# Parking two residual blocks in DRAM from the weights' queue, in program order, in a macaron decoder layer

## The chip, the cores and the metric

The kernel runs on one core of a Trainium2 chip. The metric is the device time of one execution in microseconds (us): three runs of the kernel before took 1733.95, 1736.27 and 1739.5, so the median is 1736.27. The profile is of one further execution, recorded by the hardware profiler; its times are counted from the start of its span.

Engines are named as the profile names them: PE is TensorE's matmul, PEld its load of the stationary operand, DVE is VectorE, ACT is ScalarE, POOL is GpSimd, SP is SyncE. SP issues DMAs only, and its queue carries the weights. POOL issues DMAs too, in a queue of its own. L845 is line 845 of the kernel before.

## What is computed

A decoder layer on x of 256 rows by 2048 columns in float32: half a SwiGLU, a mixer (gated linear attention in 4 heads beside dilated attention in 8), and half a second SwiGLU, each on the RMS norm of x and each added to x. The change is in the second SwiGLU.

```python
def rms_norm(x, g):
    y = x * lax.rsqrt(jnp.mean(x * x, axis=-1, keepdims=True) + EPS)
    return y * g

def swiglu(x, w_gate, w_up, w_down):          # 2048 -> 5632, twice, and 5632 -> 2048
    return (jax.nn.silu(x @ w_gate) * (x @ w_up)) @ w_down

x = x + 0.5 * swiglu(rms_norm(x, ffn1_norm), ffn1_w_gate, ffn1_w_up, ffn1_w_down)
z = rms_norm(x, mix_norm) @ w_in
...
x = x + jnp.concatenate([o_g, o_a], axis=-1) @ w_out
x = x + 0.5 * swiglu(rms_norm(x, ffn2_norm), ffn2_w_gate, ffn2_w_up, ffn2_w_down)
```

## The kernel before

**Tiles.** The 256 rows are two blocks of 128 (t = 0, 1), which stay in SBUF as the tile xs (128 partitions, block, 2048 columns). The normed activations are held transposed in hh and hl: hh is the value rounded to the fast matmul type fp32r, hl what the rounding left. A product of float32 is three matmuls, L274 (high by high), L276 (high activations by low weights) and L278 (low by high), all into one PSUM bank.

**Weights.** They come from DRAM in tiles of 1 MB (raw, three buffers), by SyncE's queue, L217, one after the other for the whole kernel. ScalarE rounds each half of a tile to wh (L113), VectorE subtracts to get wl (L114); wh and wl have four buffers each. Halves are prepared up to two ahead of the matmuls that take them. A raw buffer is free for the next tile when both of its halves are split.

**Norm.** Ahead of the second SwiGLU each 512-column piece of xs is transposed into hh and hl. Pieces 0 and 1 of each block go by norm_moved: VectorE transposes 32x32 squares (L128), GpSimd moves the squares by 16 small DMAs for each piece (move_squares, L133, here hh<-us), and VectorE multiplies with the gain when they have landed (L153). Pieces 2 and 3 go by norm_block: TensorE transposes into a PSUM bank (L109), VectorE multiplies out of it (L123), and both kinds are then split (L113, L114). Row factors come from GpSimd's power (L165).

**Gate and up of the second SwiGLU.** ffn runs 11 column blocks of 512 columns. Block 0 is plain (column_pair): for each of 16 row pieces it takes a half tile of weights and issues the matmuls of both token blocks. A dictionary called extra gives work to issue ahead of a step of this loop. Blocks 1 to 10 form part of their products with seven multiplications in place of eight (L298 to L300); for these, the sums of activations (seven_forms, L316 to L322, with split to fh and fl) and of weights (L238 and those behind it) need scratch. That scratch is xs itself: xs[:, 1, :] holds the sums, and half of xs[:, 0, :] takes the squares that GpSimd moves for the transposed outputs (xs<-us, L133). So the second SwiGLU first has to save xs, the residual, in a DRAM tile named resid, and GpSimd reads it back ahead of the down projection (L465 for block 1, L470 for block 0).

**Order.** Each engine runs its instructions in one order, which the scheduler of the tile framework sets from the program and from the dependencies it sees; an instruction may so stand elsewhere than in the code. keep_in_program_order pins an instruction to its place in the program among its queue's. Whoever overwrites a part of xs has to wait until the DMA that reads it has landed: L316 for block 1, L133's moves of block 1's outputs for block 0. The first SwiGLU has a like place: load_x (L523) loads xs by SyncE's queue, L524, in program order, at steps 9 and 11.

Of the kernel before, what the change touches and what calls it, by code (L numbers as in the profile page):

```python
# [21 lines left out]
P = 128  # L22
# [5 lines left out]
NT = S // P  # L28
# [20 lines left out]
def layer_kernel(tc, x, xT, gains, gla_gate_up, gla_gate_bias, gla_out_norm, att_q_norm, att_k_norm,  # L49
                 w_ff1, w_dn1, w_mix, w_low, w_out, w_ff2, w_dn2, c_sq, c_rope, c_mask, out):  # L50

    nc = tc.nc
# [3 lines left out]
    with ExitStack() as es:  # L56
# [35 lines left out]
        xs = cst.tile([P, NT, D], F32, name="xs")  # L92
# [749 lines left out]
            eng.dma_start(out[t * P:(t + 1) * P, c * 512:(c + 1) * 512], blk)  # L842

        resid = es.enter_context(tc.tile_pool(name="dram", bufs=1, space=bass.MemoryType.DRAM)).tile([S, D], F32, name="resid")
        ffn("ffn2", done2, resid, extra={9 + t: lambda t=t: nc.gpsimd.dma_start(resid[t * P:(t + 1) * P, :], xs[:, t, :]) for t in range(NT)}, final=True)  # L845


# [73 lines left out]
```

## Time and profile before

| | |
|---|---|
| three runs, us | 1733.95, 1736.27, 1739.5 |
| profiled execution, us | 1733.12 |
| its span, us | 1731.3 |
| ACT busy, us | 940.0 (54%) |
| POOL busy, us | 442.4 (26%) |
| weight tiles of 1 MB by SP's queue | 175 + 88 + 48 + 16 |
| SP's queue, share of the 16 DMA engines' time | 55.6% |
| POOL's queue, the same | 4.3% |
| DMA rate over the span, GB/s | 207 |

The profile lists busy time by engine, the chain of work that ended last, groups of instructions with the idle time ahead of them and what ended it, and the DMA issues with their time to landing. A releaser behind "<-" is what a wait ended with. The changed place lies at about 1070 us; the down projection of the second SwiGLU ends the kernel.

### The profile page before, as it was taken

To read this page: it belongs to the slowest core of one execution; us is meant where nothing else is said; L and a number is where in the kernel's file an instruction comes from. 1 tells how busy PE (TensorE), PEld (TensorE's weight loads), DVE (VectorE), ACT (ScalarE), POOL (GpSimd) and SP (SyncE) were. 2 spreads that over 40 slices of the span, in tenths; PEclk is the share of its full clock that TensorE was granted. 3 is DMA by queue.
4 is the path that set the end of the run, shared out by engine and by line. 5 is a ranking of instruction groups with operands and counts; after the bars stand their busy time and mean duration, and the time that the engine had idled before them with its cause. 6 is when DMAs were issued, how large, how long until landed. Compare 5 with 4: busy or idle time off the path is not lost.

```text
span 1731.3 us, 22229 instructions
## 1 busy us (share of the span) xinstructions
PE 1718.3 (99%) x8064; PEld 1498.8 (87%) x8064; DVE 1371.3 (79%) x1643; ACT 940.0 (54%) x1172; POOL 442.4 (26%) x876
## 2 busy tenths in 40 slices
PE   9999999999999999999999998999999999999999
PEld 7888888888888888888888887888888888888887
DVE  6888888888988787566655656788888898897875
ACT  7555555555555555565654544555555555565453
POOL 0333344443400701111000034333333333420000
PEclk9999999999999999999999999999999999999999
DMA  8666566566666666555444466565666655675663
GB/s 342 221 219 229 207 219 221 209 217 233 246 248 218 208 216 239 191 197 216 152 164 170 146 215 222 211 226 208 224 235 226 227 219 208 233 263 209 234 213 137
DMA packets 81710, 373.89 MB, mean 216 GB/s; under 512 B 19344, under 2 KB 36752, under 8 KB 38592
## 3 DMA queue, kind: packets, MB, share of 16 engines
q1 hardware_dynamic: 50864, 350.25, 55.6%
q0 software_dynamic: 30016, 21.16, 4.3%
q8 instruction: 63, 1.03, 0.2%
q10 hardware_dynamic: 720, 1.07, 0.2%
q14 instruction: 47, 0.39, 0.1%
HBM read 354.57 MB, written 4.19 MB: 207 GB/s over the span
## 4 chain that ended last, share of the span: by engine, by line
PE 86%; DVE 6%; DMA 5%; issue 2%; POOL 1%; ACT 1%; DVEq 0%; SPq 0%; ACTq 0%; POOLq 0%
PE acc L276 19%; PE acc L278 19%; PE acc L274 19%; PE tp L278 4%; PE tp L276 4%; PE tp L274 4%; PE acc L299 3%; PE acc L300 3%; PE acc L298 3%; DMA raw<-in_w_ff_dram 2%; DVE wl L114 2%; DMA hh<-us 2%; POOL hh L133 1%; PE tp L298 1%; PE tp L299 1%
## 5 line engine op out<-in xcount | busy, mean ns | idle before, releaser
L114 DVE TENSOR_TENSOR wl<-raw,wh 128x1024 fp32r<-128x1024 f32 (+1 forms) x658 | 790.8, 1217 | 205.8 <-ACT wh L113 201.8
L113 ACT ACTIVATE wh<-raw 128x1024 fp32r<-128x1024 f32 (+1 forms) x660 | 679.0, 1047 | 463.7 <-PE acc L278 205.5
L133 POOL DMA_DIRECT2D xs<-us x704 | 344.3, 497 | 547.5 <-issue 438.4
L276 PE MATMUL acc<-wl,hh 128*128 128x512 f32 x1232 | 372.3, 382 | 0.1
L278 PE MATMUL acc<-wh,hl 128*128 128x512 f32 x1232 | 370.3, 381 | 0.0
L274 PE MATMUL acc<-wh,hh 128*128 128x512 f32 x1232 | 364.8, 382 | 1.8 <-ACT wh L113 1.8
L274 PEld LDWEIGHTS acc<-wh,hh 128*128 128x128 f32 x1232 | 232.6, 190 | 35.4 <-ACT wh L113 2.6
L276 PEld LDWEIGHTS acc<-wl,hh 128*128 128x128 f32 x1232 | 232.9, 190 | 33.8 <-issue 1.0
L278 PEld LDWEIGHTS acc<-wh,hl 128*128 128x128 f32 x1232 | 232.5, 189 | 32.4
L278 PE MATMUL acc<-wh,ul 128*128 128x512 f32 x408 | 123.9, 379 | 0.0
L276 PE MATMUL acc<-wl,uh 128*128 128x512 f32 x408 | 123.9, 379 | 0.0
L274 PE MATMUL acc<-wh,uh 128*128 128x512 f32 x408 | 120.0, 379 | 0.2 <-ACT wh L113 0.2
L133 POOL DMA_DIRECT2D hh<-us x128 | 62.1, 501 | 141.8 <-DVE xs L487 70.5
L274 PEld LDWEIGHTS acc<-wh,uh 128*128 128x128 f32 x408 | 77.1, 189 | 11.4 <-ACT wh L113 0.6
L276 PEld LDWEIGHTS acc<-wl,uh 128*128 128x128 f32 x408 | 77.2, 189 | 10.9
L278 PEld LDWEIGHTS acc<-wh,ul 128*128 128x128 f32 x408 | 77.2, 189 | 10.9
L165 POOL TENSOR_TENSOR rs<-a,mhalf 128x4 f32<-128x4 f32 (+1 forms) x12 | 17.5, 1454 | 256.5 <-DVE a L596 256.5
L238 DVE TENSOR_TENSOR xs<-raw 128x1024 f32<-128x1024 f32 x40 | 48.2, 1206 | 33.5 <-DMA raw<-in_w_ff_dram 33.5
L113 ACT ACTIVATE wh<-xs 128x1024 fp32r<-128x1024 f32 x40 | 42.1, 1054 | 58.7 <-DVE xs L238 51.0
L274 PE MATMUL tp<-wh,hh 128*128 128x512 f32 x240 | 73.2, 379 | 0.0
L276 PE MATMUL tp<-wl,hh 128*128 128x512 f32 x240 | 71.4, 379 | 0.0
L278 PE MATMUL tp<-wh,hl 128*128 128x512 f32 x240 | 71.4, 379 | 0.0
(278 smaller groups left out, 2251.8 us busy)
## 6 DMA issues: line engine op xcount, KB each, us to landing
raw<-in_w_ff_dram SPq DMA_DIRECT2D x175, 1024.0 KB, 5.0
raw<-in_w_dn_dram SPq DMA_DIRECT2D x88, 1024.0 KB, 4.8
raw<-in_w_mix_dram SPq DMA_DIRECT2D x48, 1024.0 KB, 4.7
raw<-in_w_out_dram SPq DMA_DIRECT2D x16, 1024.0 KB, 4.8
xs<-us POOLq DMA_DIRECT2D x704, 16.0 KB, 3.6
xs<-in_x_dram SPq DMA_DIRECT2D x2, 1024.0 KB, 11.0
xs<-in_x_dram POOLq DMA_DIRECT2D x2, 1024.0 KB, 6.3
hh<-us POOLq DMA_DIRECT2D x128, 16.0 KB, 3.6
```

Of the source, the lines that this page charges most:

```text
L113: nc.scalar.activation(dst_h, src, AF.Copy)
L114: nc.vector.tensor_sub(dst_l, src, dst_h.bitcast(F32))
L133: nc.gpsimd.dma_start(dst[32 * q:32 * q + 32, r * P:(r + 1) * P], src[32 * r:32 * r + 32, q * P:(q + 1) * P])
L165: nc.gpsimd.tensor_tensor(dst, src, mhalf[:, :src.shape[-1]], op=ALU.pow)
L238: nc.vector.tensor_add(room["sum"], b1, mid)
L274: nc.tensor.matmul(ps[j], lhsT=sh, rhs=alt(wh[:, j, :]), start=first and i == 0, stop=False)
L276: nc.tensor.matmul(ps[j], lhsT=sh, rhs=alt(wl[:, j, :]), start=False, stop=False)
L278: nc.tensor.matmul(ps[j], lhsT=sl, rhs=alt(wh[:, j, :]), start=False, stop=last and i == len(ws) - 1)
L298: nc.tensor.matmul(bank, lhsT=a[0], rhs=alt(ws[0][:, j, :]), start=start, stop=False)
L299: nc.tensor.matmul(bank, lhsT=a[0], rhs=alt(ws[1][:, j, :]), start=False, stop=False)
L300: nc.tensor.matmul(bank, lhsT=a[1], rhs=alt(ws[0][:, j, :]), start=False, stop=stop)
```

## The change

The two writes of xs to resid are issued by SyncE's queue, pinned in program order, at steps 11 and 13 of block 0; before, GpSimd's queue issued them at steps 9 and 10, unpinned.

```diff
-        ffn("ffn2", done2, resid, extra={9 + t: lambda t=t: nc.gpsimd.dma_start(resid[t * P:(t + 1) * P, :], xs[:, t, :]) for t in range(NT)}, final=True)
+        ffn("ffn2", done2, resid, extra={11 + 2 * t: lambda t=t: tc.keep_in_program_order(
+            nc.sync.dma_start(resid[t * P:(t + 1) * P, :], xs[:, t, :])) for t in range(NT)}, final=True)
```

On SyncE, around the start of the second SwiGLU (raw is a weight tile, in_w_ff_dram the gate and up weights, x7 seven in a row):

```order
 L217 DMA raw<-in_w_mix_dram 128x2048 x24
 L217 DMA raw<-in_w_out_dram 128x2048 x16
-L217 DMA raw<-in_w_ff_dram 128x2048 x88
+L217 DMA raw<-in_w_ff_dram 128x2048 x7
+L846 DMA resid<-xs 128x2048
+L217 DMA raw<-in_w_ff_dram 128x2048
+L846 DMA resid<-xs 128x2048
+L217 DMA raw<-in_w_ff_dram 128x2048 x80
```

The writes stand behind the seventh and the eighth weight tile of the second SwiGLU; on GpSimd they stood behind the norm's last moves and the two powers of L165.

On VectorE, in block 0, where the last norm piece (hf, hl) is followed by the first sums of activations (L316, into xs); wl is the low half of a half tile of weights, split from raw and wh:

```order
 L123 TENSOR_TENSOR hf_8988<-tp_8983,gT_71 128x512
+L114 TENSOR_TENSOR wl_9042<-raw_9039,wh_9041 128x1024
 L114 TENSOR_TENSOR hl_80<-hf_8988,hh_79 128x4x128
+L114 TENSOR_TENSOR wl_9061<-raw_9039,wh_9060 128x1024
+L114 TENSOR_TENSOR wl_9079<-raw_9076,wh_9078 128x1024
+L114 TENSOR_TENSOR wl_9095<-raw_9076,wh_9094 128x1024
+L114 TENSOR_TENSOR wl_9113<-raw_9110,wh_9112 128x1024
+L114 TENSOR_TENSOR wl_9130<-raw_9110,wh_9129 128x1024
 L316 TENSOR_TENSOR xs_78<-hh_79,hl_80 128x256 x2
-L114 TENSOR_TENSOR wl_9042<-raw_9039,wh_9041 128x1024
```

Six splits, one ahead of the last hl and five behind it, now stand ahead of the first sums; before, they stood between and behind them.

On VectorE, in one of the ten blocks with seven products, where the first sum of a weight tile (L238, into xs) is formed; swl is the low half of a smaller piece of the same tile:

```order
 L114 TENSOR_TENSOR wl_11135<-raw_11122,wh_11134 128x1024
 L114 TENSOR_TENSOR wl_11147<-raw_11144,wh_11146 128x1024
+L114 TENSOR_TENSOR wl_11163<-raw_11144,wh_11162 128x1024
 L238 TENSOR_TENSOR xs_78<-raw_11178 128x1024
-L114 TENSOR_TENSOR wl_11163<-raw_11144,wh_11162 128x1024
 L114 TENSOR_TENSOR swl_9264<-raw_11178,swh_9263 128x512
 L114 TENSOR_TENSOR wl_11182<-raw_11178,wh_11181 128x1024
```

One split has moved from behind the sum to ahead of it; in the same blocks the split of ul (L114) has moved behind two evacuations of accumulators.

## The prediction

> **What bounds the kernel now.** I read first the busy times on the page, then the chain that ended last, then who waited for whom, and last the stretches around the changed place.
>
> ```profile
> span 1731.3 us, 22229 instructions
> PE 1718.3 (99%) x8064; PEld 1498.8 (87%) x8064; DVE 1371.3 (79%) x1643; ACT 940.0 (54%) x1172; POOL 442.4 (26%) x876
> ...
> PE 86%; DVE 6%; DMA 5%; issue 2%; POOL 1%; ACT 1%; DVEq 0%; SPq 0%; ACTq 0%; POOLq 0%
> ```
>
> TensorE is busy for all but 13.0 us, and 86% of the chain is TensorE. A change that leaves its matmuls alone can only win what TensorE now loses. In the list of waits TensorE has one entry, and it lies beside the changed lines; the timeline of TensorE shows it, and a table of stretches shows what follows it.
>
> ```profile
> PE tp L109 <- DVE hf L123: 4.4, 1, 4.4
> ...
> 1070.33 0.59 PE L278 MATMUL acc<-wh,hl 128*128 128x512 f32 x2
> 1075.27 1.09 PE L109 MATMUL tp<-ident,xs 128*128 128x128 f32 x4 [4.35 <-DVE hf L123]
> ...
> core 0: us, PE busy (x) PEld busy (x) DVE busy (x) ACT busy (x) POOL busy (x), PEclk, DMA share, GB/s
> ...
> 1070.90:1075.30 4.40, 0.05 (x2) 0.06 (x1) 1.47 (x3) 0.74 (x2) 0.83 (x2) 0.96 1.03 423
> 1075.30:1078.70 3.40, 3.40 (x13) 2.92 (x14) 3.30 (x6) 1.72 (x3) 0.00 (x0) 0.55 0.61 255
> 1078.70:1103.60 24.90, 24.90 (x118) 21.81 (x117) 20.13 (x30) 14.34 (x16) 0.00 (x0) 1.00 0.53 185
> 1103.60:1512.00 408.40, 408.38 (x1891) 357.21 (x1890) 359.28 (x404) 224.10 (x251) 158.30 (x324) 1.00 0.62 222
> 1512.00:1731.30 219.30, 215.15 (x997) 188.20 (x995) 169.16 (x196) 108.47 (x113) 14.95 (x31) 1.00 0.59 211
> ```
>
> TensorE stands still for 4.4 us, then runs 3.4 us at a granted clock of 0.55, which costs (1 - 0.55) x 3.4 = 1.5 us more. The place costs **5.9 us**, 0.34% of the run. Behind it TensorE misses 0.02 us in 433 us; what is missing at the end is the output. So 5.9 us and some tenths are all that can be won, and the question is whether the residual's writes have a part in this stall. The chain around it, and GpSimd's own timeline:
>
> ```profile
> 1065.94 2.62 issue
> 1068.55 0.43 POOL hh L133
> ...
> 1069.04 4.41 DMA hh<-us
> ...
> 1073.83 0.69 DVE hf L153
> 1074.53 0.61 DVE hf L123
> ...
> 1070.60 1.13 POOL L845 DMA_DIRECT2D resid<-xs  x2
> ```
>
> The last moves of the norm (L133) are issued at 1068.55 and 1069.04 and land 4.41 us later; the multiply of L153 waits for them, the one of L123 stands behind it, and the transposes of L109 wait for that one's bank. The residual's writes are issued at 1070.60, after all of this.
>
> **The change part by part.** *Taken from GpSimd:* two issues, 1.13 us together. GpSimd's next move (L133) is at 1105.76 after 34.02 us of waiting (row below), so nothing waits for these 1.13 us: 0.
>
> ```profile
> 1105.76 4.43 POOL L133 DMA_DIRECT2D xs<-us  x9 [34.02 <-ACT sg L426]
> ...
> 1068.12 0.33 SPq L217 DMA_DIRECT2D raw<-in_w_ff_dram  x1
> 1084.28 0.33 SPq L217 DMA_DIRECT2D raw<-in_w_ff_dram  x1
> ...
> 19.28 0.34 SPq L217 DMA_DIRECT2D raw<-in_w_ff_dram  x1
> 19.67 0.43 SPq L524 DMA_DIRECT2D xs<-in_x_dram  x1
> ...
> resid<-xs POOLq DMA_DIRECT2D x2, 1024.0 KB, 6.0
> xs<-in_x_dram SPq DMA_DIRECT2D x2, 1024.0 KB, 11.0
> ```
>
> *Given to SyncE:* the first write stands behind the seventh weight tile of the second SwiGLU, the one issued at 1068.12. It has no wait that is still open (its waits are for moves and loads of the first SwiGLU, and its rows of xs are complete before the norm whose last moves go at 1068.55), so it leaves at once, 0.4 us later, as the loads of x did at 19.67: about 1068.5, that is 2.1 us *earlier* than before, and in the weights' queue. The next weight tile is held by its buffer until 1084.28, so the issue itself (0.43) costs 0.
>
> *The moves that the stall hangs on.* Now 1 MB stands at 1068.5 in the other queue, while the last two moves wait for the DMA engines. If they have to let it pass, the stall grows by 1 MB at the 423 GB/s of the stretch 1070.90:1075.30, 1048576 / 423e3 = **2.5 us**. Bounds: 0 and +2.5; below zero a reason excludes a gain, since the writes stood behind these moves in one queue, were issued 1.6 us later, and the weights ahead are the same. How two queues share is seen in the packets (queue: packets, MB, share), for the windows 1069.5:1071.9, 1072:1073, 1118.3:1121.4 and 1121.4:1122.4; q1 is SyncE's queue, q0 GpSimd's:
>
> ```profile
> q1 hardware_dynamic: 138, 1.00, 102.3%
> ...
> q0 software_dynamic: 129, 0.30, 86.0%
> ...
> q1 hardware_dynamic: 116, 0.95, 86.9%
> q0 software_dynamic: 9, 0.00, 0.4%
> ...
> q1 hardware_dynamic: 55, 0.32, 77.6%
> q0 software_dynamic: 155, 0.08, 27.2%
> ...
> 1117.50 4.87 SPq L217 DMA_DIRECT2D raw<-in_w_ff_dram  x3
> ```
>
> While one weight tile runs (1.00 and 0.95 MB), GpSimd's queue gets next to nothing; when it ends, its moves go in a burst. At 1121.4 that happens although the next tile's issue lies between 1117.50 and 1122.37 and its packets already run in the same window (55 of q1 beside 155 of q0). So moves wait for the tile that is running, not for the one behind it. I take +0.0, near this row, and keep +2.5 for the range. The Trainium skill has this as a rule (page "DMA: Bandwidth & Descriptors", section "Queues, rings and completion order"): each DMA engine takes turns between the queues it has work for, and changes over when a packet of several descriptors is drained. By that rule the moves go first at 1072 and the sum is +0.0; without it the sum is +2.5; the four windows agree with it.
>
> *The second write* stands behind the eighth tile, so behind 1084.28. In the new order six splits, the halves of three tiles, go ahead of the sums of L316, which need it landed. Without the two L316 (0.67 us from start to the next start) and the L320 and L319 (0.40) ahead, that tile's buffer is free some 1.1 us sooner, 1083.2, and the write leaves at 1083.6. It lands, with the 6.0 of the resid row and 2.5 for the tile ahead, at about 1092.1; with the 11.0 of the x loads at 1094.6. VectorE reaches L316 after the sixth split, which ends at 1091.4 in the trace:
>
> ```profile
> 1080.82 0.76 DVE L316 TENSOR_TENSOR xs<-hh,hl 128x256 f32<-128x256 f32 x2
> 1081.49 1.22 DVE L114 TENSOR_TENSOR wl<-raw,wh 128x1024 fp32r<-128x1024 f32 x1
> 1082.63 0.28 DVE L320 TENSOR_TENSOR xs<-xs 128x128 f32<-128x128 f32 x1
> ...
> 1083.03 1.22 DVE L114 TENSOR_TENSOR wl<-raw,wh 128x1024 fp32r<-128x1024 f32 x1
> 1090.18 1.22 DVE L114 TENSOR_TENSOR wl<-raw,wh 128x1024 fp32r<-128x1024 f32 x1
> ...
> 1098.84 0.59 PE L276 MATMUL acc<-wl,hh 128*128 128x512 f32 x2
> ```
>
> So L316 waits 0.7 to 3.2 us. Behind it on VectorE stand the rest of the sums and the seventh split, whose low half TensorE takes at 1098.84. From landing to that split's end it takes 0.67 + 0.40 + 0.2 + 1.22 = 2.5 us, so the write may land as late as **1096.3** before TensorE waits: 4.2 us and 1.7 us of room. Cost on the path: 0, and one for one past 1096.3.
>
> *The rest of the second SwiGLU.* In each block VectorE now splits one more tile before the sum of L238, for whose weights it waits:
>
> ```profile
> 1323.57 1.23 DVE L238 TENSOR_TENSOR xs<-raw 128x1024 f32<-128x1024 f32 x1 [1.73 <-DMA raw<-in_w_ff_dram]
> ...
> 1316.83 0.89 PE L298 MATMUL tp<-wh,fh 128*128 128x512 f32 x2
> ```
>
> That split (1.22) fits in the wait of 1.73, and its buffer comes free sooner. TensorE shows a hitch there in one place: two matmuls from 1316.83 take 0.89 where other pairs take 0.59. The gain lies between 0 and ten blocks x 0.30 = 3.0; the stretch 1103.60:1512.00 misses only 0.02, so I take 0.3. A loss of the same size can't be excluded where other pieces moved (the split of ul now follows two evacuations): -0.3 to +0.3 again.
>
> **Sum.** Against the profiled execution's 1733.12 us (span 1731.3 and 1.8 around it): 0 (GpSimd) + 0 (SyncE) + 0.0 (moves) + 0 (L316) - 0.3 (blocks) = 1732.8. The three runs shown have their median 3.15 us above the profiled execution, so about **1736.0** in their terms.
>
> **Rivals.** *A, the stall goes:* without GpSimd's writes the moves land 4.4 us sooner, TensorE does not stop and its clock does not fall: 1736.3 - 5.9 = 1730.4. For it: the writes are the neighbours of the stall in queue and time. Against it: they are issued behind the moves, and the moves' 2.62 us hold on GpSimd ends before them. The Trainium skill (page "TensorE: Matmul & The Clock Gate", section "Part 1: The HAM clock gate") lets the clock fall after one idle window of about 3.4 us; by that figure, an estimate, a stall cut by 1.0 us would give back the 1.5 us too, and the row of 0.55 behind 4.4 us agrees as far as it goes. *B, slower: the first write cuts in.* Place: the weights' queue at 1068.5. Price: 2.5 us on the stall. It decides if the moves' packets go behind the write's, that is if they land past 1073.5. Time 1736.3 + 2.5 = 1738.8. For it: the write is issued 0.5 us before the last move. Against it: the burst at 1121.4. *C, slower too: the second write lands past 1096.3.* It takes 12.7 us from its issue instead of 8.5; one tile more ahead of it than the 11.0 of the x loads (+2.5) makes 1097.1, 0.8 us of stall, and past 3 us the clock falls as well: some 1737 to 1741. *D, the change does not take effect:* SyncE's order shows both writes there, so this has no chance of its own.
>
> **How the numbers follow.** Forecast 0.79, A 0.07, B 0.09, C 0.05. Own range of the forecast: 1733 to 1739.5, since three runs of one kernel spread from 1733.95 to 1739.5. With B and C and half of the way to A: 1731.0 to 1741.0. A measurement of this kernel tells about 0.3% (5.2 us) from no change. A alone passes that on the fast side: 0.07. On the slow side only C's end and B and C together do: 0.06. The rest, 0.87, is within.
>
> **What would show it.** In the changed profile: the two resid issues on SyncE at about 1068.5 and 1083.6; the stall before L109 again 4.4 us, the last moves landing at 1073.4 (B: at 1075.9, A: no stall); L316 waiting for a DMA for 0.7 to 3.2 us with TensorE running through 1098; TensorE without gaps from 1079 to the end. The forecast is wrong if TensorE has a second wait in its list, or if the one there changed by more than 2.5 us.

## The result and the profile after

| | before | changed |
|---|---|---|
| median of 20 runs each, us | 1735.58 | 1739.51 |
| lowest and highest, us | 1732.99, 1739.5 | 1737.83, 1741.23 |
| profiled execution, us | 1733.12 | 1739.58 |

The ratio of the changed kernel to the one before is **1.0025**, with a 95% interval of 1.0018 to 1.0031: 0.25% slower, 1735.58 x 0.0025 = 4.3 us (3.1 to 5.4). That is within the 0.3% of the forecast's "same" and inside its range, but with twenty runs on each side it is a loss and not nothing, and the mechanism is rival B's, to which 0.09 was given. The page of the changed kernel opens like the one before:

```profile
span 1737.5 us, 22235 instructions
...
PE 1719.6 (99%) x8064; PEld 1498.2 (86%) x8064; DVE 1373.2 (79%) x1643; ACT 940.4 (54%) x1172; POOL 441.4 (25%) x874
...
PE 87%; DVE 5%; DMA 4%; issue 2%; ACT 1%; POOL 1%; DVEq 0%; SPq 0%; ACTq 0%; POOLq 0%
```

TensorE's work is the same to 1.3 us; the span grew by 6.2, so 4.9 us of it went into TensorE's waits. The list of waits (engine, line, who ended it: us in total, times, longest) has the old entry, larger, and a new one on VectorE:

```profile
DVE xs L316 <- DMA resid<-xs: 2.0, 1, 2.0
...
PE tp L109 <- DVE hf L123: 7.5, 1, 7.5
```

The stretches, cut at the new places of the stall, in the same columns as before:

```profile
core 0: us, PE busy (x) PEld busy (x) DVE busy (x) ACT busy (x) POOL busy (x), PEclk, DMA share, GB/s
...
1070.90:1078.40 7.50, 0.20 (x1) 0.00 (x0) 1.23 (x3) 0.51 (x1) 0.36 (x1) 0.87 0.68 245
1078.40:1083.00 4.60, 4.39 (x15) 3.75 (x16) 4.44 (x8) 1.96 (x4) 0.00 (x0) 0.50 0.01 4
1083.00:1103.60 20.60, 20.60 (x97) 18.05 (x96) 14.68 (x22) 11.39 (x12) 0.00 (x0) 0.99 0.61 218
1103.60:1512.00 408.40, 407.65 (x1887) 356.25 (x1886) 361.26 (x403) 227.28 (x255) 156.59 (x320) 1.00 0.62 223
```

The stall went from 4.4 to 7.5 us. The clock then stands at 0.50 for 4.60 us, which costs (1 - 0.50) x 4.6 = 2.3 where it cost 1.5 before. In the blocks with seven products TensorE misses 0.75 us where it missed 0.02. Together 3.1 + 0.8 + 0.7 = 4.6 us, against 4.3 by the ratio. Some 1.6 us of the 6.2 between the two profiled executions are not placed by these rows; the medians, 3.9 apart, do not ask for them. Each of these sizes is from one profiled execution, and the two small ones are less sure than the stall. In both_13, a run described below, a stall of 4.2 us was followed by more half clock than here, some 2.6 us of cost:

```profile
1074.40:1079.60 5.20, 5.16 (x17) 4.36 (x18) 4.36 (x8) 2.54 (x5) 0.00 (x0) 0.50 0.01 3
```

The chain of waits, in order of time, and what SyncE issued:

```profile
1069.65 7.13 DMA hh<-us
...
1077.17 0.69 DVE hf L153
1077.86 0.61 DVE hf L123
...
1078.61 1.08 PE tp L109 x4
```

```profile
1068.30 0.33 SPq L217 DMA_DIRECT2D raw<-in_w_ff_dram  x1
1068.93 0.33 SPq L846 DMA_DIRECT2D resid<-xs  x1
1087.27 0.33 SPq L217 DMA_DIRECT2D raw<-in_w_ff_dram  x1
1087.65 0.42 SPq L846 DMA_DIRECT2D resid<-xs  x1
```

It is the old chain, with the last move 7.13 us on its way where it was 4.41. What each transfer took is read from the DMA issues of a short stretch, here of the changed kernel: the seventh tile (issued at 1068.30), the first write (1068.93), the two last moves (1069.17 and 1069.65), and the eighth tile (1087.27):

```profile
raw<-in_w_ff_dram SPq DMA_DIRECT2D x1, 1024.0 KB, 6.3
...
resid<-xs SPq DMA_DIRECT2D x1, 1024.0 KB, 8.2
...
hh<-us POOLq DMA_DIRECT2D x1, 16.0 KB, 6.6
...
hh<-us POOLq DMA_DIRECT2D x1, 16.0 KB, 7.1
...
raw<-in_w_ff_dram SPq DMA_DIRECT2D x1, 1024.0 KB, 6.9
```

and of the kernel before, the seventh tile and the last move:

```profile
raw<-in_w_ff_dram SPq DMA_DIRECT2D x1, 1024.0 KB, 5.0
...
hh<-us POOLq DMA_DIRECT2D x1, 16.0 KB, 4.4
```

So before, the tile was through at 1068.12 + 5.0 = 1073.1, and the last move at 1069.04 + 4.4 = 1073.4, 0.3 behind it. Now the tile is through at 1068.30 + 6.3 = 1074.6 and the last move at 1069.65 + 7.1 = 1076.8, 2.2 behind it, but ahead of the write's end at 1068.93 + 8.2 = 1077.1. The moves lose 3.4 us in **two parts**: 1.5 because the running tile is slower (0.2 of it was issued later), 1.9 because the moves then share with the write. That they share is seen in the packets of the changed kernel (queue: packets, MB, share), in the window 1073.9:1076.9; q1 is SyncE's queue, q0 GpSimd's:

```profile
q1 hardware_dynamic: 130, 0.89, 72.3%
q0 software_dynamic: 88, 0.03, 5.4%
```

The two moves are the 0.03 MB of q0, spread over the time in which the write runs.

### The profile page after: what moved, and what is told of

Its sections match the earlier page's. It is cut to its first block, busy times and chain, and to the rows that moved or that the text cites. A ratio compares the mean times of both kernels' runs of the same rounds, so it can differ in the third digit from the quotient of the medians.

```text
span 1737.5 us, 22235 instructions
## 1 busy us (share of the span) xinstructions
PE 1719.6 (99%) x8064; PEld 1498.2 (86%) x8064; DVE 1373.2 (79%) x1643; ACT 940.4 (54%) x1172; POOL 441.4 (25%) x874
## 4 chain that ended last, share of the span: by engine, by line
PE 87%; DVE 5%; DMA 4%; issue 2%; ACT 1%; POOL 1%; DVEq 0%; SPq 0%; ACTq 0%; POOLq 0%
PE acc L276 19%; PE acc L278 19%; PE acc L274 19%; PE tp L278 4%; PE tp L276 4%; PE tp L274 4%; PE acc L299 4%; PE acc L300 4%; PE acc L298 3%; DVE wl L114 2%; DMA raw<-in_w_ff_dram 2%; DMA hh<-us 1%; PE tp L298 1%; PE tp L299 1%; PE tp L300 1%
## 5 line engine op out<-in xcount | busy, mean ns | idle before, releaser
L114 DVE TENSOR_TENSOR wl<-raw,wh 128x1024 fp32r<-128x1024 f32 (+1 forms) x658 | 791.6, 1218 | 207.1 <-ACT wh L113 203.5
L165 POOL TENSOR_TENSOR rs<-a,mhalf 128x4 f32<-128x4 f32 (+1 forms) x12 | 17.4, 1454 | 256.5 <-DVE a L596 256.5
L238 DVE TENSOR_TENSOR xs<-raw 128x1024 f32<-128x1024 f32 x40 | 48.2, 1206 | 24.0 <-DMA raw<-in_w_ff_dram 23.9
```

The lines of the kernel that those rows point to most:

```text
L114: nc.vector.tensor_sub(dst_l, src, dst_h.bitcast(F32))
L165: nc.gpsimd.tensor_tensor(dst, src, mhalf[:, :src.shape[-1]], op=ALU.pow)
L238: nc.vector.tensor_add(room["sum"], b1, mid)
```

## The experiments

*Theory 1:* the first write costs all of it, by standing in the other queue when the last moves want to be served; where it was put decides, not that it is SyncE's. *Theory 2:* the new order of work on VectorE costs it (the splits ahead of L316 and L238, and L316's wait for the second write). Ratios are to runs of the kernel before on the same chip; the stall is TensorE's wait ahead of L109.

| run | median, us | ratio, 95% interval | stall, us |
|---|---|---|---|
| first_sp | 1737.68 | 1.0015 (1.0006 to 1.0024) | 7.4 |
| second_sp | 1734.89 | 1.0000 (0.9991 to 1.0009) | 4.3 |
| both_13 | 1734.97 | 0.9996 (0.9987 to 1.0005) | 4.2 |
| both_11 | 1743.56 | 1.0043 (1.0030 to 1.0056) | 11.0 |
| read_there | 1738.10 | 1.0015 (1.0005 to 1.0026) | 5.5 |
| pe_before | 1733.88 | 0.9986 (0.9974 to 0.9998) | none; 2.6 elsewhere |
| pe_after | 1732.93 | 0.9981 (0.9971 to 0.9992) | 0.4 |
| pe_13 | 1729.21 | 0.9964 (0.9951 to 0.9978) | none |

### One write each

first_sp moves the first write alone, second_sp the second alone; the other stays with GpSimd (`gp` and `sp` stand for the issue as before and as in the change):

```diff
-extra={11 + 2 * t: lambda t=t: sp(t) for t in range(NT)}
+extra={10: lambda: gp(1), 11: lambda: sp(0)}
...
-extra={11 + 2 * t: lambda t=t: sp(t) for t in range(NT)}
+extra={9: lambda: gp(0), 13: lambda: sp(1)}
```

> Only the first write (block 0 of xs) goes by SyncE, behind the seventh weight tile; the second stays with GpSimd, behind the last moves. Theory 1, order of issue: a move waits for the 1 MB transfers issued before it by the other queue, and the write at 1068.93 is ahead of the last two moves at 1069.17 and 1069.65. It expects the stall of TensorE ahead of L109 at 7.5 us as with the whole change (4.4 before), L153's moves landing at about 1076.8, and the time 3 to 5 us above the kernel before. Theory 2, the order of work on VectorE and the wait of L316 for the second write: it expects a stall of 4.4 and a time within 1 us of before, since L316 does not wait here.

> Only the second write (block 1 of xs) goes by SyncE, behind the eighth weight tile; the first stays with GpSimd, behind the last moves. Theory 1 expects the stall ahead of L109 back at 4.4 us and the time within 1 us of before, whatever L316 waits for. Theory 2 expects the stall at 4.4 too, but the time 3 to 4 us above before, with the loss spread over the blocks behind.

The waits of first_sp, and then of second_sp:

```profile
PE tp L109 <- DVE hf L123: 7.4, 1, 7.4
```

```profile
PE tp L109 <- DVE hf L123: 4.3, 1, 4.3
DVE xs L316 <- DMA resid<-xs: 2.4, 1, 2.4
```

The first write brings the stall alone, with no wait at L316. The second brings L316's wait alone, longer than with the whole change (2.4 against 2.0), and its ratio is 1.0000, to 0.09%. Theory 2 expected the opposite in both times. first_sp's time is somewhat lower than theory 1 wanted (2.5 us, 1.0 to 4.2 by its interval, expected 3 to 5). So the first write carries the stall; that it carries all of the 4.3 us is likely, but a rest of some tenths for the second write and the order on VectorE is not excluded.

second_sp also shows the slow tile by itself. Its eighth tile was issued at 1082.56 with the write behind it at 1082.94, and no moves were under way:

```profile
raw<-in_w_ff_dram SPq DMA_DIRECT2D x1, 1024.0 KB, 6.8
```

### Where in the queue

both_13 puts both behind the eighth tile, long after the moves; both_11 puts both behind the seventh:

```diff
-extra={11 + 2 * t: lambda t=t: sp(t) for t in range(NT)}
+extra={13: lambda: (sp(1), sp(0))}
...
-extra={11 + 2 * t: lambda t=t: sp(t) for t in range(NT)}
+extra={11: lambda: (sp(0), sp(1))}
```

> Both writes go by SyncE, behind the eighth weight tile, which is held by its buffer until about 1084: block 1 first, block 0 behind it. The last moves are issued long before. Theory 1 expects the stall ahead of L109 at 4.4 us or up to 0.3 less (no writes behind the moves now), and the time from 1 us below before to 1 us above. Theory 2 expects the time 3 to 4 us above before, as the work on VectorE is ordered as with the change.

> Both writes go by SyncE, one right behind the other, behind the seventh weight tile: twice as much stands ahead of or beside the last moves. Theory 1a, the queues take turns once the tile is through, so the moves (two of 16 KB) wait for a fixed number of the writes' packets: stall 7.5 us as with the change, time 3 to 5 us above before. Theory 1b, strictly by issue: the last move (1069.65) is behind the second write as well (about 1069.4), so the stall grows by another 2.5 us to about 10 us, and the time is 6 to 8 us above before. Theory 2 expects no change of the stall from 4.4.

both_13 does what theory 1 said: stall 4.2, time as before, though both writes are SyncE's and L316 stands behind the same splits. It also settles rival A: no write stands near the moves there, and 4.2 of the 4.4 us remain. So it isn't the queue as such, it is the place.

In both_11 the stall is 11.0, by its size what theory 1b gave, but for a reason that neither had. VectorE's timeline:

```profile
1079.89 0.76 DVE L316 TENSOR_TENSOR xs<-hh,hl 128x256 f32<-128x256 f32 x2 [11.72 <-DMA resid<-xs]
1080.57 0.68 DVE L153 TENSOR_TENSOR hf<-hh,gT 128x512 f32<-128x512 f32 x1
```

The scheduler has put the first L316, which waits for the second write, ahead of L153. GpSimd's timeline has the two last moves, and the DMA issues the last one's time:

```profile
1068.31 0.98 POOL L133 DMA_DIRECT2D hh<-us  x2 [2.60 <-issue]
```

```profile
hh<-us POOLq DMA_DIRECT2D x1, 16.0 KB, 7.3
```

The second of them, issued at about 1068.8, was there at 1076.1; the multiply could have run 4.4 us before its 1080.57, and 11.0 - 4.4 = 6.6 would have been the stall. That is nearer to theory 1a's 7.5 than to 10, but not a clean test of 1b, since the moves' issue began ahead of both writes here. What speaks against "strictly by issue" is the changed kernel: its last move, issued behind the write, landed 0.3 us ahead of it.

The border isn't sharp either. In both_11 the last move's issue began 0.04 us ahead of the first write's (1068.79 and 1068.83), and yet it landed 1.3 us behind the tile (1068.20 + 6.6 = 1074.8). In first_sp the first of the two moves was issued 0.31 us ahead of the write (1070.57 and 1070.88) and landed 0.7 us behind the tile, the other, issued 0.17 us behind the write, 1.7 us behind it.

### A read in the write's place

read_there is the kernel before with one transfer more, from x into an SBUF tile that nothing reads; the tile's pool is closed ahead of the first block with seven products:

```diff
+                if final:
+                    idle = spare.enter_context(tc.tile_pool(name=name + "i", bufs=1, reuse_waits="tile")).tile([P, 2048], F32, name="idle")
+                    extra = {**extra, 11: lambda: tc.keep_in_program_order(nc.sync.dma_start(idle, x[0:P, :]))}
...
+                        spare.close()
```

> The kernel before with one more transfer: a read of 1 MB of x from DRAM into unused SBUF, on SyncE behind the seventh weight tile, where the change has its first write; the writes stay with GpSimd. Theory 1, taking turns: once the seventh tile is through, the two last moves share the DMA engines with whatever 1 MB was issued ahead of them. It expects them 1 to 2.5 us later than before behind their tile's end (0.35 us in the kernel before, 1.9 to 2.2 with a write there), a stall of 5.5 to 7.5 us and a time 1.5 to 4 us above before. The rival, that it takes a write to DRAM: with a read the moves land 0.4 us behind the tile's end and the stall stays at 4.4. What both leave open: with the change the seventh tile itself took 6.3 us from issue to landing where it took 5.0 before; if that comes from a write behind a read, it takes 5.0 here.

The tile, issued at 1067.34, the first move (1067.37, ahead of the read at 1067.72) and the last (1067.85, behind it):

```profile
raw<-in_w_ff_dram SPq DMA_DIRECT2D x1, 1024.0 KB, 5.2
hh<-us POOLq DMA_DIRECT2D x1, 16.0 KB, 5.3
...
hh<-us POOLq DMA_DIRECT2D x1, 16.0 KB, 6.0
```

Tile at 1072.5, moves at 1072.7 and 1073.85: the first passes, the last comes 1.3 us behind the tile, where before it came 0.3 behind. The stall is 5.5, 1.1 more than before, at the lower edge of what theory 1 gave; the rival's 4.4 falls. So sharing needs no write. The slow tile does: 5.2 here, against 6.3 to 6.9 with a write behind it (6.3 and 6.9 in the changed kernel, 6.7 in first_sp, 6.8 in second_sp, 6.6 in both_13 and both_11, 6.5 in pe_13 below).

### Taking the moves off the path

The last moved piece of the norm goes through TensorE instead, in the kernel before (pe_before), in the changed one (pe_after), and with both_13's writes (pe_13):

```diff
-        later.append(lambda: (norm_moved if c < 2 else norm_block)(t, c, gi))
+        later.append(lambda: (norm_moved if c < 2 and (gi, t, c) != (2, 1, 1) else norm_block)(t, c, gi))
```

> The kernel before, with the last of the moved norm pieces (block 1, columns 512 to 1023, of the norm ahead of the second SwiGLU) transposed by TensorE (norm_block) in place of VectorE and GpSimd's moves: 48 moves instead of 64, four transposes more on TensorE. Theory 1: the stall hangs on the moves alone, so it goes from 4.4 to under 1.5 us, TensorE keeps its clock, and the time is 3 to 5 us below before. The rival, that something else is late there as well (the splits of the norm, or the weights): the stall stays above 3 us and the time within 1.5 us of before.

> The changed kernel, with the same last piece transposed by TensorE. Theory 1: the first write costs only through the last moves it holds back; with these issued some 5 us earlier and not late, the writes' queue no longer matters: the time is within 1 us of the kernel with the writes on GpSimd and the same piece on TensorE, so 2 to 5 us below before and 6 to 9 us below the changed kernel. Theory 2, the order on VectorE and the wait of L316: the 3 to 4 us between the two kernels stay.

> The last moved norm piece transposed by TensorE, and both writes by SyncE behind the eighth weight tile, block 1 first, since L316 waits for block 1 alone. Theory 1: no stall behind the norm, and L316 waits less than the 4.3 us it waited with the changed order of writes and the same piece on TensorE; the time is 0 to 1.5 us below that kernel, so 2.5 to 5 us below before. The rival, that two writes in a row hold up the weights (a tile with a write behind it took 6.3 to 6.9 us where 5.0 is usual): TensorE waits for weights of the next tiles, and the time is 1 us or more above that kernel.

In pe_before the stall ahead of L109 is gone, but TensorE waits elsewhere; its timeline there, and the stretches around it:

```profile
1072.14 0.70 PE L276 MATMUL acc<-wl,hh 128*128 128x512 f32 x2 [2.60 <-DVE wl L114]
```

```profile
1069.50:1072.10 2.60, 0.04 (x1) 0.00 (x0) 1.91 (x4) 1.40 (x2) 0.00 (x0) 1.00 0.01 3
1072.10:1076.00 3.90, 3.86 (x18) 3.41 (x19) 3.90 (x8) 0.80 (x2) 0.00 (x0) 1.00 0.37 78
```

With the norm done earlier, L316 comes earlier too and waits 2.3 us for GpSimd's second write, with the split that TensorE needs behind it. That is a new wait in place of the old, which theory 1 had left out (it said under 1.5), and the time is 2.4 us below the kernel before (0.3 to 4.5), where 3 to 5 were expected. The clock stays at 1.00 after 2.6 us. In pe_after the splits stand ahead of L316; it waits 4.3 us there and TensorE hardly notices. In this trace the changed order of VectorE is even of use. The times of pe_before and pe_after, 1733.88 and 1732.93, don't tell the two apart, so the 4 us that the change costs are gone. Theory 2 expected them to stay.

pe_13 goes on from there. L316 waits 1.2 us, and TensorE is busy throughout:

```profile
1055.00:1103.60 48.60, 48.60 (x233) 42.32 (x233) 36.61 (x53) 24.50 (x33) 5.34 (x11) 1.00 0.67 236
```

It takes 1729.21 us, 0.36% below the kernel before (0.22 to 0.49%), or 6.2 us by the ratio where 2.5 to 5 were expected; by the two ratios it is some 10 us below the changed one. Its ratio is the lowest of all, though from five runs and with an interval that meets pe_after's, and it holds both writes in the weights' queue.

## Why the prediction was wrong

**The step that failed** is the one on the moves: "So moves wait for the tile that is running, not for the one behind it. I take +0.0". The burst at 1121.4 was read as if its moves had passed a tile that was queued ahead of them. They had not. In the kernel before, the next tile was issued at 1119.77; the move ahead of it (1119.54) and one behind it (1120.51) took, beside that tile:

```profile
1119.77 0.33 SPq L217 DMA_DIRECT2D raw<-in_w_ff_dram  x1
...
raw<-in_w_ff_dram SPq DMA_DIRECT2D x1, 1024.0 KB, 5.9
xs<-us POOLq DMA_DIRECT2D x1, 16.0 KB, 4.1
...
xs<-us POOLq DMA_DIRECT2D x1, 16.0 KB, 5.3
```

The first landed at 1123.6, in the burst; the second at 1125.8, when the next tile was through (1125.7). The burst held only moves that had been issued ahead of the tile behind. The prediction's other burst, the window 1072:1073, is no support either: no tile stood behind the running one there (the next was issued at 1084.28), and of the 0.30 MB in GpSimd's queue the last two moves, 16 KB each, are 0.03; nearly all the rest is GpSimd's first write. By the order of issue a write at 1068.5 stands ahead of moves at 1068.55 and 1069.04, and B, not +0.0, was the likeliest: some 1738.8, against 1739.5 measured. "It decides if the moves' packets go behind the write's" was the right question, and the row that answers it was in the trace.

**B's price was too small**, and with it the upper end: 2.5 us for the stall, 3.1 measured. B also left out the half clock, another 0.8 in these two profiles, a size that varies by as much with a stall of the old length (both_13). The 1 MB at 423 GB/s priced only the sharing (1.9 measured); nothing stood for the tile that a write behind it slows, 1.3 us beyond its later issue.

**The rule of the Trainium skill** (page "DMA: Bandwidth & Descriptors", section "Queues, rings and completion order"), turns between the queues, agrees with these runs in that the two last moves landed at 1075.8 and 1076.8, inside the write's time. What was drawn from it, "by that rule the moves go first", did not come: the first of them landed 1.2 us behind the tile's end, where before it was 0.2, and the other 1.0 us later. Each of them waited for a share of the write.

**GpSimd's issues and SyncE's time, 0:** right. The writes left at 1068.93 and 1087.65, forecast 1068.5 and 1083.6; the second is late with the stall and with the slower tiles.

**The second write, 0:** right, and second_sp tests it. L316 waited 2.0 us (0.7 to 3.2 were given), TensorE ran on. The write landed 8.9 us after its issue where 8.5 were forecast, at 1096.6; that is past the forecast's 1096.3, but the whole place had moved back by some 3 us, and the 12.7 us that rival C asked for were not reached.

**The blocks, -0.3:** the sign is doubtful. TensorE misses 0.75 us there instead of 0.02. In the same stretch of the other profiles it misses 0.09 (first_sp), 0.19 (both_11), 0.38 (both_13) and 0.59 us (second_sp), so it doesn't come with the stall; second_sp's time shows no loss to 0.09%. Whether the order of VectorE costs some tenths stays open.

**Rival A:** the writes on GpSimd had no part in the old stall (both_13). Its remark that a shorter stall would keep the clock holds in pe_before: 1.00 after 2.6 us, 0.55 after 4.4. The Trainium skill's figure of about 3.4 us (page "TensorE: Matmul & The Clock Gate", section "Part 1: The HAM clock gate") lies between the two. Rival C's "past 3 us" lies there too; no run here has a stall between 2.6 and 4.2 us.

## What to carry to other kernels

Before a bulk transfer is moved to another queue, list by time of issue what small transfers are under way and whether the path hangs on them: the transfer delays those issued just behind it, though they stand in another queue, and here some that were issued up to 0.3 us ahead of it. When a burst in a trace seems to overtake, compare the times of issue before using it as a rule. And a wait that a change moves is harmless only with the work behind it on its engine: the same L316 cost nothing behind six splits, 2.6 us ahead of one that TensorE needed, and 4.4 us ahead of the norm.

## What the hardware showed that was not expected

A write to DRAM that is queued behind a read, in one queue, slows the read: a 1 MB tile took 6.3 to 6.9 us with the write 0.4 to 0.6 us behind it (seven tiles in six kernels) and 5.2 with a read there. It took 5.0 in the kernel before, where only GpSimd's writes follow it, 2.5 us later and in the other queue, and 4.8 for the same tile in both_13, with no write near it. In pe_after, with other tiles just ahead, two tiles with a write behind them took 8.2 and 9.5. The packets show it before the tile has landed (1074.6), here from 1071.0 to 1073.6 in the changed kernel, and from 1070.5 to 1072.4 in the one before:

```profile
DMA packets 98, 0.74 MB, mean 284 GB/s; under 512 B 8, under 2 KB 8, under 8 KB 8
```

```profile
DMA packets 124, 0.79 MB, mean 414 GB/s; under 512 B 13, under 2 KB 29, under 8 KB 29
```

Why the rate falls is open. A write from a queue other than the read's did not do the same at 2.5 us behind it (the 5.0 us of the kernel before); at 0.4 to 0.6 us it was not tried.
